# Strassen's seven products for most pairs of MLP up tiles in a two-layer float32 encoder

## The chip, the cores and the metric

One Trainium2 chip (trn2), one core of it. The metric is the device time of one execution in microseconds. Before the change three runs took 1248.66, 1249.28 and 1248.66 us, median 1248.66. TensorE (PE in the profile) multiplies matrices, VectorE (DVE) and ScalarE (ACT) work element by element, GpSimd (POOL) and SyncE (SP) here set buffers and issue DMAs.

## The reference

A two-layer encoder on 512 tokens of 1024 channels, in float32. Each layer normalises x, projects it, runs four mixers side by side (an S5 state-space scan, a convolution module and two kinds of attention), projects their outputs back into x, and then runs the gated MLP that this change is about:

```python
h = rms_norm(x, attn_norm_g[i])
proj = h @ w_in[i]                      # four mixers read slices of proj
...
x = x + mixed @ w_out[i]
h = rms_norm(x, ffn_norm_g[i])
x = x + conv_ffn(h, ffn_w_up[i], ffn_conv_w[i], ffn_conv_b[i], ffn_w_down[i])

def conv_ffn(h, w_up, conv_w, conv_b, w_down):
    u = depthwise_conv(h @ w_up, conv_w, conv_b)      # width 3 over the tokens
    gate, up = jnp.split(u, 2, axis=-1)
    return (jax.nn.silu(gate) * up) @ w_down
```

w_up has 1024 x 5632 values a layer, w_down 2816 x 1024. A last RMSNorm closes the trunk.

## The kernel before

**Layout.** x lies transposed in SBUF, as eight tiles of 128 channels x 512 tokens (`xs_`). A weight tile is the stationary operand, 128 x 128 of it at a time; a tile of activations, 512 tokens wide, is the moving one. All large products are made in three TensorE products of the type fp32r: each operand is split into a rounded part hi and a remainder lo, and hi*hi, hi*lo and lo*hi are summed in PSUM (`mm3`). A weight tile is loaded by SyncE, its hi is a copy by ScalarE or VectorE (`copy` leaves the choice to the planner), its lo a VectorE subtraction (`wget`).

**The MLP** (`ffn`, from line 1392). 44 up tiles a layer, in 22 pairs of one gate and one up tile. `up_tile` takes 8 slices of channels x 3 products of 512 columns into one PSUM bank. The moving operand is x times the norm's gain; the norm's reciprocal root r, which is the same for all channels of a token, is multiplied in when the bank is read (`evac_r`), so that products start before r is known. Then come the conv (one ScalarE operation with the middle tap and the bias, two VectorE taps), Silu of the gate, the product of both, and its split into hi and lo (`pair`). The down projection (`down`) runs in parts of the 22 tiles, `PARTS = (5, 6, 6, 5)`: for each part, eight output tiles with 3 products per tile of the part, each ending in an addition to x by VectorE. A part's down products are recorded after the second pair of the next part. The last part of layer 1 (`finish`) runs in two halves of 256 tokens, with the last norm and the stores behind each half. In layer 0 each pair is followed by a piece of `s5_prep`, small VectorE operations that prepare constants of the next layer's scan.

**The order of the work.** The program first records all instructions and then issues them in the order of a list schedule (`_Plan`). `_cost` (from line 547) gives each instruction a duration, `LAT` the delay between engines; `forward` picks for each engine, in simulated time, the ready instruction with the highest priority (its distance to the end), and lets it start only where its buffers fit. Ten passes are made, forward and backward in turn, and the shortest is issued. At run time each engine works off its list strictly in that order; waits between engines follow from the data and the buffers.

**Buffers.** SBUF has an arena of `NSLOT` = 49 slots of 515 words a partition, one of `NBIG` = 19 slots of 1024 words, and small ones. `CAPS` limits how many raw, hi and lo weight tiles may live at once (3, 5, 5). PSUM has eight banks of 512 words. All waits of SyncE's queue for a free slot hold the loads behind them.

Of the kernel before, what the change touches and what calls it, by code (L numbers as in the profile page):

```python
# [17 lines left out]
P = 128  # L18
# [3 lines left out]
KT = D // P  # L22
DFF = 2816
NPAIR = DFF // P
PARTS = (5, 6, 6, 5)
OUTP = ((3,), (0, 1, 2))
CAPS = (3, 5, 5)
ORDER = ("SGCMpsgcym", "SGCMsgcym")
EARLY = (4, 5)
CONV_PE = ((True, True), (True, False))  # L30
# [22 lines left out]
    CST[_n] = (_off, _w)  # L53
    _off += _w
CSTW = _off
NSLOT = 49
NBIG = 19
SLOTW = S + 3
XW = S + 32
# [7 lines left out]
class _Ap:  # L67
# [17 lines left out]
        return self._do("bitcast", d)  # L85

    def window(self, dims, offset):
        """A view with its own strides."""
        return _Ap(self.base, self.chain + (("window", (dims, offset), {}),), _window(self.proto, dims, offset))

    def unsqueeze(self, d):
# [27 lines left out]


class _Plan:
    """Records instructions, then issues them in the order of a list schedule.

    Buffers live in arenas of SBUF and in the banks of PSUM from their first write to their last use;
    Tile derives every wait from the order of issue."""

    SETS = {"Exp": "exp", "Ln": "ln", "Tanh": "exp", "Sigmoid": "sig", "Silu": "silu", "Gelu_apprx_tanh": "gelu",
            "Sin": "silu"}
# [69 lines left out]
        return op  # L198

    def tiled(self, mms):  # L200
        """Matrix products in column tiles of the array, which run side by side."""
        d = max(_cost("T", *m)[4] for m in mms) + 53.0 * (len(mms) - 1)
        return self.add([("T", "group", mms, {}, d, 0.0, 0.0)])

# [35 lines left out]
            b.at = at  # L240

    def settle(self):
        """Classes of the buffers where the instructions run in the order of recording."""
        left, users, home = dict(self.limit), {}, {}
        for op in self.ops:
            for b in op.bufs:
                users[b] = users.get(b, 0) + 1
        for op in self.ops:
            for b in op.bufs:
                if b not in home:  # L250
                    home[b] = "b" if b.space == "s" and not left["s"] else b.space
                    left[home[b]] -= 1
                    if left[home[b]] < 0:
                        raise RuntimeError("the buffers do not fit: " + home[b])
            for b in op.bufs:
                users[b] -= 1
                if not users[b]:
                    left[home[b]] += 1
        return home
# [45 lines left out]
        return tail  # L305

    def forward(self, prio, ref, home, horizon):
        """One list schedule. ref is an order that fits the buffers: an instruction may run ahead of it
        only where the rest of ref still fits, so that no schedule gets stuck."""
        import bisect  # L310
        import heapq

# [45 lines left out]
            return z <= a or int(load[c][a:z].max()) + k <= limit[c]  # L358

        def fits(op):  # L360
            """The classes for the buffers that op would take, or None."""
            got, need, upto = [], {}, {}
            lag = pos[op.idx] - head
            for b in op.outs:
# [183 lines left out]
def _cost(e, fn, a, k):  # L548
    n = _free(a[0])
    dma = 0.0  # L550
    if e == "T":
        if fn == "transpose":
            d = 109.0
        elif a[1].proto.dtype == F32R:
            d = max(n, 256) / 2.4 + 3.0
        else:
            d = 4.0 * max(n, 128) / 2.4 + 4.0
    elif e == "V":
        ps_ = any(_psum(z) for z in a)
        if fn == "tensor_reduce":  # L560
            d = 65.0 + 1.04 * _free(a[1])
        elif fn == "reciprocal":
            d = 70.0 + 8.0 * n
        elif fn == "memset":
            d = 60.0 + 0.5 * n
        elif fn == "tensor_copy":
            d = 65.0 + (1.04 if ps_ else 0.52) * n
        elif fn == "tensor_scalar":
            d = (125.0 if isinstance(a[2], _Ap) else 65.0) + (1.04 if ps_ else 0.52) * n
        elif fn == "scalar_tensor_tensor":  # L570
            d = (130.0 if isinstance(a[2], _Ap) else 68.0) + 1.04 * n
        else:
            d = 68.0 + 1.04 * n
    elif e == "A":
        d = (65.0 if _psum(a[1]) else 95.0) + 0.82 * n
        if isinstance(k.get("bias"), _Ap):
            d += 90.0
        if isinstance(k.get("scale"), _Ap):
            d += 90.0
        if "accum_out" in k:  # L580
            d += 90.0
    elif e == "G":
        d = 110.0 + (2.0 if fn == "scalar_tensor_tensor" else 1.3) * n
    else:
        d = 470.0 if a[0].shape[0] == P and a[1].shape[0] == P else 640.0
        dma = max(90.0, a[0].shape[0] * n * 4 / 359.0)
    return (e, fn, a, k, d, (2000.0 + dma) if dma else 0.0, dma)
# [3 lines left out]
def trunk_kernel(  # L591
# [30 lines left out]
    xs_ = const.tile([P, KT, S], F32, name="xs_")  # L622
    fing_ = const.tile([P, KT], F32, name="fing_")
    vec_ = const.tile([P, L, VECW], F32, name="vec_")
    slots = ctx.enter_context(tc.tile_pool(name="slots", bufs=1))
    banks = [psp.tile([P, S], F32, name=f"bank{i}") for i in range(8)]
    plan = _Plan(tc, slots, {"s": NSLOT, "b": NBIG, "t": 16}, banks, c_sb)
# [29 lines left out]
    for k in range(KT):  # L657
        lead.append(X.dma_start(x[k], xT[k * P:(k + 1) * P, :]))
    fing = plan.fixed(fing_[:, :])
    X.dma_start(fing, fin_g)  # L660

    vecs = {}
# [8 lines left out]

    def wget(src, n, cap=True):
        raw = sb(F32, (P, n), ("raw", CAPS[0]) if cap else None)
        hi = sb(F32R, (P, n), ("whi", CAPS[1]) if cap else None)
        lo = sb(F32R, (P, n), ("wlo", CAPS[2]) if cap else None)
        plan.loaded = X.dma_start(raw, src)
        copy(hi, raw)
        V.tensor_sub(lo, raw, hi.bitcast(F32))
        return hi, lo
# [38 lines left out]
        return acc  # L718

    def colsum(acc, mat=None):  # L720
        """Sums over the partitions, in every partition."""
        p_ = ps(acc.shape)
        T.matmul(p_, ones if mat is None else mat, acc)
        return p_
# [375 lines left out]
        return [v_[:, :, 0:64], v_[:, :, 64:128]]  # L1100

    def attend(scores, vt):
        """Two heads; their outputs side by side in the partitions."""
        pt = [[b4(F32, (P, 2, S)) for _ in range(2)] for _ in range(2)]
        tot = tiny((P, 4, 2))
        for hh in range(2):
# [31 lines left out]
        return y  # L1138

    def group_norm(l, grp, y):  # L1140
        """y is the group, but twice that for group 0."""
        r = rstd(sumsq(y), 1024 if grp == 0 else 256)
        g, o = tiny((P, 2)), VEC["mix_g"][0] + 2 * grp
        V.tensor_scalar(g, vecs[l][:, o:o + 2], 1.0 if grp else 0.5, None, ALU.mult)
# [12 lines left out]
    def mixing(l):  # L1157
# [224 lines left out]
        for grps in OUTP:  # L1382
# [3 lines left out]
            for m in range(KT):  # L1386
# [2 lines left out]
                mm3(p_, w, range(n), mh, ml, P, P)  # L1389
                V.tensor_add(x[m], x[m], p_)  # L1390

    def ffn(l, side):
        xh, xl, r = prenorm(l, "ffn_g")
        fw, _ = VEC["fc_w"]
        fb, _ = VEC["fc_b"]

        def up_tile(i):
            w = wget(w_up[l, i], KT * P)
            p_ = ps()
            mm3(p_, w, range(KT), xh, xl, P, P)  # L1400
            u = evac_r(p_, r)

            def cw(k):
                return vecs[l][:, fw + 3 * i + k:fw + 3 * i + k + 1]

            y = s2()
            A.activation(y, u, AF.Identity, scale=cw(1), bias=vecs[l][:, fb + i:fb + i + 1])
# [2 lines left out]
            return y  # L1410

        def pair(j):
            g_ = up_tile(2 * j)
            u_ = up_tile(2 * j + 1)
            A.activation(g_, g_, AF.Silu)
            V.tensor_mul(g_, g_, u_)
            return split(g_)
# [11 lines left out]
                V.tensor_add(x[m], x[m], p_)  # L1429

        def finish(k0, n):
            """The last part of the last layer and the norm after it, in two halves of the tokens."""
            ph = {k: prods[k0 + k][0] for k in range(n)}
            pl = {k: prods[k0 + k][1] for k in range(n)}
            H = S // 2
# [22 lines left out]
        pend = None  # L1458
        for n in PARTS:
            for j in range(n):  # L1460
                prods.append(pair(base + j))
                next(side, None)
                if j == 1 and pend is not None:
# [162 lines left out]
```

## Time and profile before

| | before |
|---|---|
| median of three runs | 1248.66 us |
| span of the profiled execution, first to last instruction | 1248.9 us |
| mean granted TensorE clock | 0.998 |
| busy: PE, DVE, ACT, POOL | 1222.4, 926.8, 615.2, 6.9 us |
| TensorE products | 5824 |
| HBM read | 118.96 MB |

The page gives no time of the profiled execution beside its span; the span stands for it. PE's busy time counts pipelined products from start to modelled end, so that a busy PE need not be at its fastest; the count of products in a window gives their rate. "PEld" are weight loads, which overlap products. The rows of a group end with the idle time just before its instructions and what ended it. Nearly every instruction is issued by one helper, so that all rows carry the line L527 and are told apart by operation, shape and buffer: `bank` is PSUM, `v_s` a slot of the small arena, `v_b` of the large one, `xs__65` is x, `vec__67` the vector of gains and taps, `c_sb` constants. The MLP of layer 0 lies at about 267 to 640 us, that of layer 1 from about 870 us to the end. A few per cent of the product records can be missing.

### The profile page before, as it was taken

What the parts mean: (1) busy time and instruction counts of PE and PEld (TensorE: products, weight loads), DVE (VectorE), ACT (ScalarE), POOL (GpSimd) and SP (SyncE); (2) the same over time, 40 slices, a digit from 0 to 9 for tenths busy, and PEclk for the clock granted to TensorE, in tenths of its full rate; (3) what the DMA queues carried; (4) which work ended last, traced back from release to release, by engine and by line L of the source; (5) the groups of instructions that cost most, each with busy time, mean ns of one, the idle gap of its engine ahead of it and who ended that gap; (6) DMA issues with size and microseconds to landing.
All of it is one profiled execution on the core that took longest, in us unless ns stands there. A gap on an engine that the chain in (4) does not pass through costs nothing.

```text
span 1248.9 us, 15868 instructions
## 1 busy us (share of the span) xinstructions
PE 1222.4 (98%) x5824; PEld 937.8 (75%) x5824; DVE 926.8 (74%) x1706; ACT 615.2 (49%) x983; POOL 6.9 (1%) x27
## 2 busy tenths in 40 slices
PE   7999899999999999999999999999999999999996
PEld 5875456878888878888888756668888888888886
DVE  8889988868899665665677998887666656557465
ACT  6448689654443352333352666985533333234223
POOL 0000000000000000000000000000000000000000
PEclk9999999999999999999999999999999999999999
DMA  8559461332223332432555156234223332322211
GB/s 303 148 187 268 107 156 36 134 119 89 71 77 101 101 131 92 123 95 73 187 188 179 53 140 148 64 102 133 87 67 99 109 96 89 99 102 76 83 45 68
DMA packets 71662, 144.38 MB, mean 116 GB/s; under 512 B 20256, under 2 KB 28960, under 8 KB 71456
## 3 DMA queue, kind: packets, MB, share of 16 engines
q1 hardware_dynamic: 71584, 143.37, 37.5%
q8 instruction: 46, 0.75, 0.2%
q14 instruction: 32, 0.26, 0.1%
HBM read 118.96 MB, written 13.89 MB: 106 GB/s over the span
## 4 chain that ended last, share of the span: by engine, by line
PE 88%; DVE 5%; ACT 3%; DMA 1%; issue 1%; SPq 1%; ACTq 0%; DVEq 0%
PE bank L527 88%; DVE v_s L527 4%; ACT v_s L527 2%; DVE v_b L527 1%; DMA v_b<-v_b 1%; ACT L527 1%; SPq L527 1%; ACT v_b L527 1%; DVE v_t L527 0%; DMA xs__65<-in_xT_dram 0%; DMA v_s<-y_d 0%; ACTq L1621 0%; DVEq L1621 0%; ACTq L527 0%
## 5 line engine op out<-in xcount | busy, mean ns | idle before, releaser
L527 PE MATMUL bank<-v_s,v_b 128*128 128x512 f32 (+3 forms) x4594 | 1041.0, 396 | 11.6 <-ACT v_b L527 8.6
L527 PEld LDWEIGHTS bank<-v_s,v_b 128*128 128x128 f32 (+2 forms) x4594 | 794.8, 183 | 219.4 <-issue 25.7
L527 DVE TENSOR_TENSOR v_b<-v_b,v_b 128x1024 fp32r<-128x1024 f32 (+4 forms) x208 | 217.2, 1051 | 33.2 <-PE bank L527 18.2
L527 ACT CAST v_b<-v_b 128x1024 fp32r<-128x1024 f32 (+2 forms) x184 | 168.8, 934 | 114.8 <-PE bank L527 85.1
L527 DVE TENSOR_TENSOR v_s<-v_s,v_s 128x512 f32<-128x512 f32 (+6 forms) x294 | 179.9, 627 | 26.1 <-ACT v_s L527 23.2
L527 DVE TENSOR_TENSOR v_s<-bank,v_s 128x512 f32<-128x512 f32 (+1 forms) x119 | 83.0, 701 | 139.6 <-PE bank L527 137.5
L527 ACT ACTIVATE v_s<-v_s,vec__67 128x512 f32<-128x512 f32 x87 | 71.0, 817 | 195.3 <-DVE v_s L527 192.2
L527 DVE SCALAR_TENSOR_TENSOR v_s<-v_s,vec__67,v_s 128x511 f32<-128x511 f32 (+8 forms) x201 | 148.6, 746 | 15.3 <-ACT v_s L527 9.7
L527 ACT ACTIVATE v_s<-v_s 128x512 f32<-128x512 f32 (+2 forms) x124 | 71.1, 587 | 80.3 <-DVE v_s L527 79.4
L527 DVE TENSOR_TENSOR xs__65<-xs__65,bank 128x512 f32<-128x512 f32 x88 | 59.5, 682 | 61.5 <-PE bank L527 61.5
L527 ACT CAST v_s<-v_s 128x512 fp32r<-128x512 f32 (+1 forms) x70 | 40.0, 585 | 72.9 <-DVE v_s L527 71.4
L527 ACT ACT_TABLE_LOAD x52 | 66.7, 1283 | 15.7 <-DVE v_s L527 7.6
L527 PE MATMUL bank<-v_b,v_b 96*128 96x512 f32 (+5 forms) x264 | 74.1, 450 | 0.0
L527 PE MATMUL bank<-c_sb,v_s 128*128 128x128 f32 x368 | 64.8, 278 | 1.3 <-ACT v_s L527 1.2
L527 PEld LDWEIGHTS bank<-c_sb,v_s 128*128 128x128 f32 x368 | 44.6, 140 | 27.5 <-issue 18.5
L527 PE MATMUL bank<-v_b,v_s 128*128 128x64 f32 (+4 forms) x268 | 60.7, 393 | 1.9 <-ACT v_s L527 1.2
L527 PE MATMUL bank<-v_s,v_s 128*64 128x128 f32 (+2 forms) x258 | 57.4, 348 | 1.4 <-ACT v_s L527 1.4
L527 ACT ACTIVATE v_s<-bank,v_t 128x512 f32<-128x512 f32 x68 | 46.5, 697 | 10.6 <-DVE v_t L527 10.5
L527 PEld LDWEIGHTS bank<-v_b,v_s 128*128 128x128 f32 (+1 forms) x268 | 34.0, 173 | 16.0 <-issue 7.7
L527 DVE TENSOR_REDUCE v_t<-bank 128x1 f32<-128x512 f32 x64 | 42.3, 681 | 4.4 <-PE bank L527 3.7
L527 PEld LDWEIGHTS bank<-v_b,v_b 96*128 96x128 f32 (+3 forms) x264 | 33.2, 165 | 16.5 <-issue 8.1
L527 PEld LDWEIGHTS bank<-v_s,v_s 128*128 128x128 f32 (+1 forms) x258 | 32.1, 165 | 14.9 <-issue 5.7
(82 smaller groups left out, 517.9 us busy)
## 6 DMA issues: line engine op xcount, KB each, us to landing
v_b<-in_w_up_dram SPq DMA_DIRECT2D x88, 512.0 KB
v_b<-in_w_in_dram SPq DMA_DIRECT2D x28, 512.0 KB
v_b<-in_w_dn_dram SPq DMA_DIRECT2D x32, 384.0 KB
v_b<-in_w_dn_dram SPq DMA_DIRECT2D x32, 320.0 KB
v_b<-v_b SPq DMA_DIRECT2D x24, 256.0 KB
v_b<-in_w_out_dram SPq DMA_DIRECT2D x16, 384.0 KB
v_s<-x_d SPq DMA_DIRECT2D x22, 257.5 KB
v_s<-wt_d SPq DMA_DIRECT2D x15, 256.0 KB
```

Source lines behind the costliest of these rows:

```text
L527: self.issued(op, getattr(eng[e], fn)(*[res(z) for z in a], **{n: res(z) for n, z in k.items()}))
```

## The change

19 of the 22 pairs of a layer (all but the first three) are computed by one level of Strassen's scheme, in the variant with chained sums. The pair of tiles (2 x 128 outputs), the 1024 channels and the 512 tokens are each halved: A is the weight in four blocks of 128 outputs x 512 channels, B the normalised activations in four blocks of 512 channels x 256 tokens. Seven block products of 4 x 3 TensorE products with 256 columns take the place of eight.

- **Weights of a pair.** SyncE loads five blocks of 128 x 512 words (two of them into the targets of sums), GpSimd adds a further block to each of two of these by a DMA with addition, VectorE makes two more sums (`s2_`, `s4`). The seven operands are split into hi and lo.
- **Activations.** Once a layer, recorded after the first pair, `operands` makes the four blocks of x times gain times r, four combinations of them, and splits all seven. r must be known for these.
- **Sums of the products.** Three banks: `xb` takes products 1, 4, 6 and 7 on top of each other and is read after each, `yb` takes 3 and 5, `zb` takes 2. Four reads are ScalarE copies, three are VectorE additions, all 256 wide. The up tile comes out with its sign reversed, and so takes negated conv taps (`nfw`, made once a layer).
- **The first three pairs** stay as they are, but with weights in blocks of 512 words instead of 1024.
- **Limits.** `PARTS` becomes (4, 4, 4, 4, 3, 3); `NSLOT` 50; `WCAPS` limits the raw, hi and lo blocks that live at once to 10, 9 and 9.
- **Planner.** The duration of an fp32r product becomes 0.4453 ns a column (at least 256) + 4 ns, before 1/2.4 + 3; a DMA of GpSimd gets a duration.

```diff
-PARTS = (5, 6, 6, 5)
+PARTS = (4, 4, 4, 4, 3, 3)
+DIRECT = 3
...
+WCAPS = (10, 9, 9)
...
-NSLOT = 49
+NSLOT = 50
...
-            d = max(n, 256) / 2.4 + 3.0
+            d = 0.4453 * max(n, 256) + 4.0
...
+    elif e == "G" and fn == "dma_start":
+        d, dma = 1300.0, 2.0 * a[0].shape[0] * n * 4 / 359.0
...
+        def operands():
+            q = {}
+            for kh, nh in ((0, 0), (0, 1), (1, 0), (1, 1)):
+                t_ = q[kh, nh] = b4(shape=(P, 4, H))
+                for k in range(4):
+                    V.scalar_tensor_tensor(t_[:, k], x[4 * kh + k][:, H * nh:H * nh + H], vcol(l, "ffn_g", 4 * kh + k),
+                                           r[:, H * nh:H * nh + H], ALU.mult, ALU.mult)
+            b11, b12, b21, b22 = q[0, 0], q[0, 1], q[1, 0], q[1, 1]
+            n1, n2, t4 = (b4(shape=(P, 4, H)) for _ in range(3))
+            V.tensor_sub(n1, b11, b12)
+            f11 = halves(b11)
+            V.scalar_tensor_tensor(n2, n1, -1.0, b22, ALU.mult, ALU.subtract)
+            fn1 = halves(n1)
+            V.scalar_tensor_tensor(t4, n2, -1.0, b21, ALU.mult, ALU.subtract)
+            f21, fn2 = halves(b21), halves(n2)
+            V.tensor_sub(b12, b22, b12)
+            return dict(b11=f11, b21=f21, n1=fn1, n2=fn2, b22=halves(b22), t3=halves(b12), t4=halves(t4))
+
+        def product(out, w, f, start):
+            for k in range(4):
+                sl = slice(k * P, k * P + P)
+                T.matmul(out, w[0][:, sl], f[0][:, k], start=start and k == 0, stop=False, skip_group_check=True)
+                T.matmul(out, w[0][:, sl], f[1][:, k], start=False, stop=False, skip_group_check=True)
+                T.matmul(out, w[1][:, sl], f[0][:, k], start=False, stop=(k == 3), skip_group_check=True)
+
+        def quarters(j):
+            src = {(i, h): w_up[l, 2 * j + i, :, 512 * h:512 * h + 512] for i in range(2) for h in range(2)}
+            a0, a1, c1, s1, s2_, s3, s4 = (sb(F32, (P, 512), ("sw", WCAPS[0])) for _ in range(7))
+            for t_, z in ((s1, (1, 0)), (s3, (0, 0)), (a0, (0, 0)), (a1, (0, 1)), (c1, (1, 1))):
+                X.dma_start(t_, src[z])
+            GP.dma_start(s1, src[1, 1], accum_op=ALU.add)
+            GP.dma_start(s3, src[1, 0], accum_op=ALU.add)
+            V.tensor_add(s2_, s1, a0)
+            V.tensor_add(s4, s2_, a1)
+            w11, w12, w1, w2, w4, w3, w22 = (halves(z, *CW) for z in (a0, a1, s1, s2_, s4, s3, c1))
+            g_, u_ = s2(), s2()
+            xb, yb, zb = (ps((P, H)) for _ in range(3))
+            product(xb, w11, ops["b11"], True)
+            A.activation(g_[:, 0:H], xb, AF.Copy)
+            product(zb, w12, ops["b21"], True)
+            V.tensor_add(g_[:, 0:H], g_[:, 0:H], zb)
+            product(yb, w1, ops["n1"], True)
+            A.activation(u_[:, H:S], yb, AF.Copy)
+            product(xb, w2, ops["n2"], False)
+            A.activation(g_[:, H:S], xb, AF.Copy)
+            product(yb, w4, ops["b22"], False)
+            V.tensor_add(g_[:, H:S], g_[:, H:S], yb)
+            product(xb, w3, ops["t3"], False)
+            V.tensor_add(u_[:, H:S], u_[:, H:S], xb)
+            product(xb, w22, ops["t4"], False)
+            A.activation(u_[:, 0:H], xb, AF.Copy)
+            return g_, u_
...
         def pair(j):
-            g_ = up_tile(2 * j)
-            u_ = up_tile(2 * j + 1)
+            g_, u_ = straight(j) if j < DIRECT else quarters(j)
+            g_ = spread(2 * j, g_, False)
+            u_ = spread(2 * j + 1, u_, j >= DIRECT)
             A.activation(g_, g_, AF.Silu)
             V.tensor_mul(g_, g_, u_)
             return split(g_)
...
         for n in PARTS:
             for j in range(n):
+                if base + j == 1:
+                    ops = operands()
                 prods.append(pair(base + j))
```

`halves` splits a tile into hi and lo, `straight` is the old up tile with its weights in halves, `spread` the conv with plain or negated taps.

More of the change, by code (lines that the diff above doesn't have):

```diff
@@ L624, in trunk_kernel @@
     vec_ = const.tile([P, L, VECW], F32, name="vec_")
+    nfw_ = const.tile([P, 6 * NPAIR], F32, name="nfw_")
     slots = ctx.enter_context(tc.tile_pool(name="slots", bufs=1))
@@ L659, in trunk_kernel @@
     fing = plan.fixed(fing_[:, :])
+    nfw = plan.fixed(nfw_[:, :])
     X.dma_start(fing, fin_g)
@@ L673, in wget, with halves @@
         raw = sb(F32, (P, n), ("raw", CAPS[0]) if cap else None)
-        hi = sb(F32R, (P, n), ("whi", CAPS[1]) if cap else None)
-        lo = sb(F32R, (P, n), ("wlo", CAPS[2]) if cap else None)
         plan.loaded = X.dma_start(raw, src)
+        return halves(raw, ("whi", CAPS[1]) if cap else None, ("wlo", CAPS[2]) if cap else None)
+    def halves(raw, ch=None, cl=None):
+        hi, lo = sb(F32R, raw.shape, ch), sb(F32R, raw.shape, cl)
         copy(hi, raw)
@@ L1390, in mixing, with blocks @@
                 V.tensor_add(x[m], x[m], p_)
+    def blocks(l, j):
+        w = [[sb(F32, (P, 512), ("sw", WCAPS[0])) for _ in range(2)] for _ in range(2)]
+        for i in range(2):
+            for h in range(2):
+                X.dma_start(w[i][h], w_up[l, 2 * j + i, :, 512 * h:512 * h + 512])
+        return w
     def ffn(l, side):
@@ L1395, in ffn @@
         fb, _ = VEC["fc_b"]
[L1397 to L1401, printed above, removed]
+        V.tensor_scalar(nfw, vecs[l][:, fw:fw + 6 * NPAIR], -1.0, None, ALU.mult)
+        H = S // 2
+        CW = ("sh", WCAPS[1]), ("sl", WCAPS[2])
+        def operands():
[15 more added lines that the diff above has]
+            return dict(b11=f11, b21=f21, n1=fn1, n2=fn2, b22=halves(b22), t3=halves(b12), t4=halves(t4))
@@ new lines, in straight @@
+        def straight(j):
+            out = []
+            for w in blocks(l, j):
+                w = [halves(z, *CW) for z in w]
+                p_ = ps()
+                for k in range(KT):
+                    sl = slice(k % 4 * P, k % 4 * P + P)
+                    wh, wl = w[k // 4]
+                    T.matmul(p_, wh[:, sl], xh[k], start=(k == 0), stop=False)
+                    T.matmul(p_, wh[:, sl], xl[k], start=False, stop=False)
+                    T.matmul(p_, wl[:, sl], xh[k], start=False, stop=(k == KT - 1))
+                out.append(evac_r(p_, r))
+            return out
@@ L1403, in cw, with spread @@
+        def spread(i, u, neg):
             def cw(k):
-                return vecs[l][:, fw + 3 * i + k:fw + 3 * i + k + 1]
+                z = 3 * i + k
+                return nfw[:, z:z + 1] if neg else vecs[l][:, fw + z:fw + z + 1]
             y = s2()
```

## The prediction

> **What bounds the kernel now.** I read the page's busy shares and chain of waits first, then windows of the MLP stage, then the groups of instructions with shapes kept apart, and last the timeline where VectorE runs without a pause.
>
> ```profile
> span 1248.9 us, 15868 instructions
> PE 1222.4 (98%) x5824; PEld 937.8 (75%) x5824; DVE 926.8 (74%) x1706; ACT 615.2 (49%) x983; POOL 6.9 (1%) x27
> PE 88%; DVE 5%; ACT 3%; DMA 1%; issue 1%; SPq 1%; ACTq 0%; DVEq 0%
> ...
> core 0: us, PE busy (x) PEld busy (x) DVE busy (x) ACT busy (x) POOL busy (x), PEclk, DMA share, GB/s
> 100.00:150.00 50.00, 47.24 (x307) 21.70 (x306) 49.40 (x157) 36.23 (x65) 0.48 (x4) 1.00 0.77 209
> 300.00:400.00 100.00, 100.00 (x432) 80.95 (x432) 90.72 (x205) 42.33 (x67) 1.78 (x5) 1.00 0.24 78
> 900.00:1000.00 100.00, 100.00 (x433) 80.91 (x432) 65.16 (x86) 37.51 (x50) 0.00 (x0) 1.00 0.30 93
> 880.00:1200.00 320.00, 320.00 (x1381) 258.94 (x1380) 198.63 (x261) 114.51 (x148) 0.00 (x0) 1.00 0.29 90
> ```
>
> TensorE makes 88% of the chain that ends last. In the MLP of layer 1 (880 to 1200 us) it never pauses, at the full granted clock of 1.00: 320 / 1381 = 231.7 ns for a product of 512 columns. VectorE has 38% of that time free. The row 300 to 400 lies in the MLP of layer 0, where VectorE also prepares the next layer's S5 constants: it is 91% busy, and TensorE still starts 432 products against 433 in layer 1. So on this plan a VectorE at 91% costs TensorE nothing. At 99% (100 to 150 us) TensorE does show gaps.
>
> **TensorE.** A pair now costs 2 x 8 x 3 = 48 products of 512 columns; a Strassen pair 7 x 4 x 3 = 84 of 256. This shape runs already, in the last step of the kernel, with the same order of hi, hi, lo weights and a weight load for each:
>
> ```profile
> 1209.75 19.56 PE L527 MATMUL bank<-v_s,v_b 128*128 128x256 f32 x164
> L527 PE MATMUL bank<-v_s,v_b 128*128 128x256 f32 x240 | 30.4, 282 | 0.0
> 1209.75:1229.31 19.56, 19.56 (x167) 19.56 (x166) 10.78 (x25) 4.54 (x11) 0.00 (x0) 1.00 0.00 1
> 1212.00:1220.00 8.00, 8.00 (x70) 8.00 (x69) 5.16 (x12) 2.45 (x6) 0.00 (x0) 1.00 0.00 0
> ```
>
> The run of 164 ends with the last one's own 0.28 us, of which 0.12 would be its slot: (19.56 - 0.16) / 164 = 118.3 ns. Bounds: 8.00 / 70 = 114.3 (the count holds products begun before the window) and 19.56 / 164 = 119.3. A pair goes from 48 x 231.7 = 11.12 us to 84 x 118.3 = 9.94, that is 1.18 us less (1.10 to 1.52 by the bounds). 38 pairs: **45.0 us** (42 to 58). A layer's MLP on TensorE, with 528 products of the down projection, goes from 1584 x 231.7 = 367 us to 672 x 231.7 + 1596 x 118.3 = 344.5.
>
> In that last step the weight loads are busy for 19.56 of 19.56 us, against 81 of 100 us with 512 columns: at 256 columns the load is nearly as long as the product. The Trainium skill, "TensorE: Matmul & The Clock Gate" (LDWEIGHTS; and under Part 3, what overlaps), gives 128 columns of weights 107 ns and says that a load overlaps running products only when its row group differs. By that rule as it stands a product of 256 columns would take over 213 ns and the change would lose some 38 x (84 x 0.213 - 11.12) = 257 us. The trace differs, with 118.3 ns in this same shape, so I give that outcome no more than 1 in 100, within the 0.07 of the accumulates below.
>
> **VectorE.** Mean durations, and the interval at which independent instructions follow each other:
>
> ```profile
> L527 DVE TENSOR_TENSOR v_b<-v_b,v_b 128x1024 fp32r<-128x1024 f32 x114 | 138.4, 1217 | 7.5 <-PE bank L527 6.3 <-issue 0.4 <-ACT v_b L527 0.2
> L527 DVE SCALAR_TENSOR_TENSOR v_s<-v_s,vec__67,v_s 128x511 f32<-128x511 f32 x166 | 122.7, 747 | 11.5 <-ACT v_s L527 9.7
> L527 DVE TENSOR_TENSOR v_s<-v_s,v_s 128x512 f32<-128x512 f32 x154 | 103.5, 685 | 6.4 <-ACT v_s L527 4.0 <-PE bank L527 0.9
> L527 DVE TENSOR_TENSOR v_s<-xs__65,bank 128x256 f32<-128x256 f32 x16 | 6.4, 418 | 8.3 <-PE bank L527 8.3
> ...
> 1013.73 2.35 DVE L527 TENSOR_TENSOR v_b<-v_b,v_b 128x1024 fp32r<-128x1024 f32 x2
> 1211.24 0.74 DVE L527 SCALAR_TENSOR_TENSOR v_s<-v_s,vec__67,v_s 128x511 f32<-128x511 f32 x1
> 1211.91 0.68 DVE L527 TENSOR_TENSOR xs__65<-xs__65,bank 128x512 f32<-128x512 f32 x1
> 1212.50 0.69 DVE L527 TENSOR_TENSOR v_s<-v_s,v_s 128x512 f32<-128x512 f32 x1
> 1218.01 0.42 DVE L527 TENSOR_TENSOR v_s<-xs__65,bank 128x256 f32<-128x256 f32 x1
> 1218.34 1.48 DVE L527 TENSOR_TENSOR v_s<-v_s,v_s 128x256 f32<-128x256 f32 x3
> 1241.99 3.25 DVE L527 SCALAR_TENSOR_TENSOR v_s<-v_s,fing__66,v_s 128x256 f32<-128x256 f32 x8 [2.27 <-ACT v_s L527]
> ```
>
> Intervals: 0.60 us for a 512-wide two-tensor operation (1211.91 to 1212.50), 0.67 for a conv tap, 2.35 - 1.22 = 1.13 at 1024, 0.33 for a 256-wide add from PSUM, 0.40 for a 256-wide scale. Each is about 0.08 under the mean duration. Now, a layer takes 44 x (1.13 + 0.60 + 2 x 0.67) + 22 x 1.2 + 45 for down = 206 us by intervals, or 229 with 284 x 0.08 added; the window gives 198.63 / 320 x 367 = 228. So unpressed VectorE counts mean durations, and the intervals are what it can be pressed to.
>
> A Strassen pair has 11 operations 512 wide (2 weight sums, 7 lo parts, the product, its lo part), 3 adds from PSUM and 4 taps: 6.6 + 1.0 + 2.7 = 10.3 us, against 7.3 for a pair now. A layer then has 19 x 10.3 = 196; 3 straight pairs of 8 operations and 4 taps, 22; down in six parts, 32 lo parts of 512 and 16 of 384 columns (0.47 from the slope) and 48 adds to x, 19 + 8 + 29 = 56 (45 before, so six parts cost 11); the seven operands, 16 scales, 4 combinations and 7 lo parts, 6 + 5 + 8 = 19; the norm 10. Sum **303 us by intervals**, 303 + 516 x 0.08 = 344 by durations, for 344.5 us of TensorE. Layer 0 has the S5 preparation on top: 90.72 - 65.16 = 25.6 in one window and about 3 before it, so 331 (372).
>
> Layer 1 is thus at 88%, below the 91% that the trace shows as free: nothing lost in its steady part. Layer 0 is at 96%. If 91% is all that TensorE tolerates, the stage takes 331 / 0.907 = 365 and loses 20 us; at 98.8% it loses nothing. I take 95%: 348, **4 us**. At each start three straight pairs (33 us of TensorE) must cover the norm's reciprocal root (some 5 us) and, on VectorE, evacuations and weight halves (3 x 3.6), operands (19) and the first halves: 5 + 11 + 19 + 1 = 36. **3 us a layer**, 0 to 8; the taps of the straight pairs can wait.
>
> At the end the last part has 3 tiles, not 5. The last pair's chain of evacuation, conv, Silu, product and split (about 6 us by the durations above) is covered by the other tiles of that part in eight banks: 8 x 2 x 3 x 0.118 = 5.7 us, before 11.3. **2 us**, 0 to 4.
>
> **ScalarE and PSUM.**
>
> ```profile
> L527 ACT CAST v_s<-v_s 128x512 fp32r<-128x512 f32 x59 | 36.3, 620 | 71.7 <-DVE v_s L527 71.4
> L527 ACT ACTIVATE v_s<-v_s,vec__67 128x512 f32<-128x512 f32 x87 | 71.0, 817 | 195.3 <-DVE v_s L527 192.2 <-issue 2.9
> L527 ACT COPY v_s<-bank 128x224 f32<-128x224 f32 x7 | 2.4, 347 | 7.2 <-PE bank L527 3.1 <-DVE v_s L527 2.6 <-issue 1.5
> ```
>
> A pair: 8 casts, 2 conv starts, 4 copies out of PSUM (0.37 each) and a Silu (0.63): 8.7 us; with down 10 of 15.5 us. No bound. Within a pair, product 4 waits for the copy that read product 1's bank, and product 7 follows product 6 in the same bank behind a VectorE add, some 1 us. Down tiles and the next pair's first product are there to fill it. Cost 0; without them 1 us x 38.
>
> **DMAs.** SyncE issues 5 loads of 256 KB a pair and GpSimd 2 that add to them; 2.25 MB per 15.5 us with down, against 1.5 MB in 16.7 us at a DMA share of 0.29. No accumulating DMA exists before. The nearest row is a plain load that a cast waited for:
>
> ```profile
> 1169.73 0.33 SPq L527 DMA_DIRECT2D v_b<-in_w_dn_dram  x1
> 1172.91 0.84 ACT L527 CAST v_b<-v_b 128x768 fp32r<-128x768 f32 x1 [1.75 <-DMA v_b<-in_w_dn_dram]
> POOL v_b L527 <- PE bank L527: 382.8, 6, 183.4
> ```
>
> 384 KB take 3.2 us from issue to use. An accumulate is at least that and, reading its target too, I bound it at twice, 6.4; so a sum is ready 6 to 10 us after its first load. Ten slots for 7 raw tiles a pair let one live 10 x 15.5 / 7 = 22 us, so I take 0. If late, the weight add at the head of VectorE's in-order queue holds the taps, splits and evacuations behind it, and TensorE with them. GpSimd's queue also holds memsets that wait long for their buffers (last row); an accumulate behind one waits too. The Trainium skill, "DMA: Bandwidth & Descriptors" (Anatomy of one DMA), has 2.0 us + bytes / 436e3, by which 256 KB is 2.6 us and the sum stays as it is; no run here shows it.
>
> **Sum.** 1248.9 - 45.0 + 4 + 6 + 2 = **1216 us**. The profiled span equals the median of the runs (1248.66) within 0.02%, so I carry it over.
>
> **Rivals.** *Full gain*: everything is hidden, 1248.9 - 45 = 1204, at the low price of a product 1191. For it: the free 91% row; against it: layer 0 at 96%.
> *VectorE becomes the bound* (slower): it works off its queue at mean durations because each pair's adds, taps and splits hang on each other. Then layer 0 needs 372 us and layer 1 344; with 5% of waits 392 + 362 = 754 against 734 now: 1269. It decides from the point where VectorE's achieved price per operation passes about 0.05 us over the interval in both layers. For it: the unpressed windows count durations; against it: 90.72 of 100 with TensorE unhurt.
> *Accumulates set the pace* (slower): GpSimd's queue takes two a pair one after the other; over 7.75 us each they are slower than TensorE's 15.5. At 8.5 us: 38 x 1.5 = 57 more than the forecast, 1273. Against it: 3.2 us for the plain load.
> *The new TensorE price mostly reorders*: the planner's list changes in every stage, and what is won in the MLP is given back in mixing. TensorE's idle time is only 26.5 us in all (1248.9 - 1222.4), so some 10 us either way around the forecast, with 30 at the far end: 1246.
>
> **How the numbers follow.** Forecast (1209 to 1230) 0.50, full gain 0.17, VectorE bound, wholly or in part (1230 to 1269), 0.20, accumulates 0.07, reordering 0.06. Of VectorE's 0.20, 0.08 stays faster, 0.04 lands within 0.2%, 0.08 is slower; the last two give 0.05 faster, 0.02 same, 0.06 slower. A measurement of this kernel can tell about 0.2% (2.5 us) from no change. So faster 0.80, same 0.06, slower 0.14. The range runs from 1201 (full gain with a little of the lower product price) to 1248.
>
> **What would show it.** In MLP windows about 118 ns per product of 256 columns and TensorE busy throughout in layer 1; VectorE near 90% in layer 1, above 93% in layer 0. Wrong if TensorE's waits in the MLP name VectorE for more than about 25 us together, if VectorE waits for an accumulating DMA, or if 256-column products come slower than 120 ns.

## The result and the profile after

The changed kernel takes 1284.24 us (median of four runs, 1282.14 to 1286.61) against 1248.97 of the kernel before on the same chip (1248.66 to 1250.99). The ratio is 1.0275 with a 95% interval of 1.0255 to 1.0295: 2.7% slower. The prediction was 1216 us, faster, with a range up to 1248. The profiled execution took 1286.61 us with a span of 1284.8, at a mean granted clock of 0.965.

From the page of the changed kernel, the span, the busy shares and the clock in 40 slices of 32 us:

```profile
span 1284.8 us, 20243 instructions
PE 1213.8 (94%) x7144; PEld 986.5 (77%) x7144; DVE 1101.0 (86%) x2167; ACT 751.7 (59%) x1363; POOL 73.0 (6%) x103
PEclk9999699999997959999999999999999999999998
```

TensorE is idle for 71.0 us instead of 26.5, and the clock leaves its full value in slices 5, 13 and 15. To see where, the span is cut into its four stages: mixing and MLP of layer 0, mixing and MLP of layer 1. The border between two stages is ScalarE's last split of x for the norm that opens the later one; the first 15 us are left out. Columns are the window, its length, busy time and count of PE, PEld, DVE, ACT and POOL, the granted clock, the DMA share and GB/s. The windows of before:

```profile
15.00:266.30 251.30, 247.33 (x1296) 167.19 (x1295) 220.92 (x498) 169.35 (x306) 3.24 (x11) 1.00 0.52 156
266.30:646.60 380.30, 380.30 (x1686) 305.98 (x1685) 276.04 (x478) 152.96 (x228) 2.83 (x7) 1.00 0.34 109
646.60:870.40 223.80, 220.14 (x1131) 157.43 (x1130) 190.94 (x371) 144.92 (x252) 0.48 (x4) 1.00 0.42 119
870.40:1248.90 378.50, 368.47 (x1704) 302.88 (x1702) 229.16 (x324) 138.00 (x186) 0.00 (x0) 0.99 0.27 86
```

and of the changed kernel:

```profile
15.00:281.50 266.50, 256.18 (x1295) 171.12 (x1294) 227.74 (x524) 166.41 (x299) 6.08 (x14) 0.96 0.52 150
281.50:689.20 407.70, 374.68 (x2383) 334.09 (x2382) 351.72 (x683) 224.63 (x430) 33.17 (x42) 0.94 0.52 142
689.20:924.20 235.00, 229.21 (x1119) 158.85 (x1118) 196.61 (x384) 149.74 (x256) 3.98 (x8) 0.99 0.42 112
924.20:1284.80 360.60, 347.59 (x2340) 318.15 (x2338) 315.24 (x546) 201.08 (x368) 29.48 (x34) 0.99 0.48 126
```

| stage | before | predicted | after | after - before |
|---|---|---|---|---|
| mixing, layer 0 | 251.3 | 251.3 | 266.5 | +15.2 |
| MLP, layer 0 | 380.3 | 364.8 | 407.7 | +27.4 |
| mixing, layer 1 | 223.8 | 223.8 | 235.0 | +11.2 |
| MLP, layer 1, and end | 378.5 | 361.0 | 360.6 | -17.9 |

The predicted column is the prediction's own terms put to their stages: 22.5 us of TensorE off each MLP, 3 us for its start, 4 more in layer 0, 2 at the end. Layer 1 comes out as forecast, though in part by errors that cancel: TensorE's busy time there fell by 20.9 us (368.47 to 347.59) where 22.5 were forecast, and its idle time grew by 3.0 where start and end were to cost 5. Layer 0's MLP misses by 43 us, and the two mixing stages, in which not one operation was changed, lose 26.

**Layer 1: the price of a product holds.** The longest run of 256-column products on the timeline of the changed kernel:

```profile
978.99 10.87 PE L529 MATMUL bank<-v_b,v_s 128*128 128x256 f32 x90
```

With the last product's slot taken off as in the prediction, (10.87 - 0.16) / 90 = 119.0 ns. The 107 ns that the Trainium skill ("TensorE: Matmul & The Clock Gate", LDWEIGHTS; Part 3, what overlaps) would put beside each product is not there; the trace contradicts that rule, as the prediction assumed. The group of these products has almost no idle time ahead of it in 925 to 1250 us:

```profile
L529 PE MATMUL bank<-v_b,v_s 128*128 128x256 f32 x1532 | 256.3, 281 | 2.1 <-ACT v_s L529 1.4 <-DVE xs__65 L529 0.5
```

The adding DMAs, which no row of before could price, from the DMA part of the page and the view of their tile, and the one wait of VectorE for any such weight:

```profile
v_s<-in_w_up_dram POOLq DMA_DIRECT2D x70, 256.0 KB, 4.8
DMA to landing us min/median/max: 3.9/4.6/9.1
DVE v_b L529 <- DMA v_b<-in_w_up_dram: 0.6, 1, 0.6
```

A median of 4.6 to 4.8 us from issue to landing lies inside the bounds of 3.2 to 6.4, but the slowest took 9.1; the 2.6 us quoted beside these bounds is under even the fastest, 3.9. VectorE waited 0.6 us for them in layer 0 and not at all in layer 1.

**Layer 0: two gaps.** Five windows of 20 us of its MLP, in the changed kernel:

```profile
361.00:381.00 20.00, 19.53 (x131) 17.77 (x130) 19.98 (x60) 12.31 (x26) 1.93 (x4) 1.00 0.52 139
381.00:401.00 20.00, 8.37 (x36) 6.81 (x35) 19.16 (x59) 7.97 (x16) 3.12 (x4) 0.73 0.53 132
421.00:441.00 20.00, 20.00 (x134) 18.26 (x132) 16.48 (x30) 9.37 (x20) 2.26 (x3) 1.00 0.30 69
441.00:461.00 20.00, 9.03 (x44) 7.06 (x42) 15.21 (x25) 8.96 (x23) 2.28 (x3) 0.59 0.40 111
461.00:481.00 20.00, 13.64 (x59) 8.93 (x59) 11.76 (x18) 5.02 (x16) 0.53 (x1) 0.50 0.17 58
```

The two gaps differ. In the first (381 to 401) VectorE is full; in the second (441 to 481) it is busy 27 of 40 us (15.21 + 11.76). The timeline of the first gap, TensorE's rows and then VectorE's (start, duration, operation, count, idle time before it and what ended it):

```profile
383.77 3.05 PE L529 MATMUL bank<-v_s,v_s 128*128 128x512 f32 x12 [0.95 <-DVE v_s L529]
397.50 2.72 PE L529 MATMUL bank<-v_b,v_s 128*128 128x256 f32 x11 [10.68 <-DVE xs__65 L529]
...
392.27 0.74 DVE L529 SCALAR_TENSOR_TENSOR v_s<-v_s,nfw__68,v_s 128x511 f32<-128x511 f32 x1
392.93 0.22 DVE L529 TENSOR_TENSOR v_b<-v_b 128x64 f32<-128x64 f32 x1
393.12 0.69 DVE L529 TENSOR_TENSOR v_b<-v_b,v_s 128x512 f32<-128x512 f32 x1
393.73 0.22 DVE L529 TENSOR_TENSOR v_b<-v_b 128x64 f32<-128x64 f32 x1
396.76 0.68 DVE L529 TENSOR_TENSOR xs__65<-xs__65,bank 128x512 f32<-128x512 f32 x1
```

TensorE waits 10.68 us for an addition to x that empties a bank. Ahead of that addition VectorE's list alternates MLP operations with the narrow ones (16 to 64 columns) of the S5 preparation. Second gap, TensorE and then SyncE's queue:

```profile
447.55 2.07 PE L529 MATMUL bank<-v_s,v_s 128*128 128x512 f32 x4 [5.44 <-DVE xs__65 L529]
470.79 1.97 PE L529 MATMUL bank<-c_sb,v_s 128*128 128x128 f32 x8 [5.51 <-ACT v_b L529]
...
419.31 21.82 SPq L529 DMA_DIRECT2D v_s<-in_w_up_dram  x6
451.71 3.00 SPq L529 DMA_DIRECT2D wt_d<-v_s  x2
479.89 1.11 SPq L529 DMA_DIRECT2D k_d<-v_b  x1
481.57 0.37 SPq L529 DMA_DIRECT2D v_s<-in_w_up_dram  x1
```

Six up weight loads are spread over 22 us to 441.1, and the next one is issued at 481.57. Between them SyncE's queue has nothing but the preparation's stores to scratch (`wt_d`, `g_d`, `k_d`) and, from 479.5 us, two loads for down. The queue itself stands for most of these 40 us: by its waits some 25 us for results that these stores take (10.5 before the first `wt_d`, 6.1 before the `k_d` at 470.40), and 8.6 us for TensorE, before the first load for down. The up loads come behind all of this in its list. TensorE starts no 256-column product from 441.6 to 483.5 us and does a few products of 512 columns and the preparation's small ones, one dependent step at a time. In this stretch the granted clock falls to 0.59 and 0.50, so that what TensorE does there takes longer as well.

### The profile page after: what moved, and what is told of

Read it like the earlier page. It is cut to its first block, busy times and chain, and to the rows that moved or that the text cites. A ratio compares the mean times of both kernels' runs of the same rounds, so it can differ in the third digit from the quotient of the medians.

```text
span 1284.8 us, 20243 instructions
## 1 busy us (share of the span) xinstructions
PE 1213.8 (94%) x7144; PEld 986.5 (77%) x7144; DVE 1101.0 (86%) x2167; ACT 751.7 (59%) x1363; POOL 73.0 (6%) x103
## 5 line engine op out<-in xcount | busy, mean ns | idle before, releaser
L529 PE MATMUL bank<-v_b,v_s 128*128 128x256 f32 (+3 forms) x3350 | 579.0, 294 | 25.9 <-DVE xs__65 L529 11.2
L529 PEld LDWEIGHTS bank<-v_b,v_s 128*128 128x128 f32 (+1 forms) x3350 | 476.5, 189 | 56.8 <-ACT v_s L529 14.7
L529 PE MATMUL bank<-v_s,v_s 128*128 128x512 f32 (+2 forms) x1462 | 441.0, 386 | 7.1 <-DVE xs__65 L529 5.4
L529 DVE TENSOR_TENSOR v_s<-v_s,v_s 128x512 fp32r<-128x512 f32 (+6 forms) x622 | 393.3, 656 | 33.7 <-ACT v_s L529 13.7
L529 PE MATMUL bank<-v_s,v_b 128*128 128x512 f32 (+3 forms) x1510 | 360.3, 421 | 11.0 <-ACT v_b L529 8.6
L529 PEld LDWEIGHTS bank<-v_s,v_s 128*128 128x128 f32 (+1 forms) x1462 | 259.2, 187 | 64.0 <-issue 6.2
L529 ACT CAST v_s<-v_s 128x512 fp32r<-128x512 f32 (+2 forms) x371 | 215.5, 605 | 156.5 <-PE bank L529 79.9
L529 PEld LDWEIGHTS bank<-v_s,v_b 128*128 128x128 f32 (+2 forms) x1510 | 225.9, 176 | 93.1 <-issue 34.2
L529 PE MATMUL bank<-v_b,v_b 128*128 128x256 f32 (+5 forms) x382 | 113.4, 398 | 4.9 <-DMA v_b<-v_b 2.0
L529 DVE SCALAR_TENSOR_TENSOR v_s<-v_s,vec__67,v_s 128x511 f32<-128x511 f32 (+9 forms) x131 | 97.2, 746 | 8.6 <-ACT v_s L529 6.4
```

The source lines that it names most:

```text
L529: self.issued(op, getattr(eng[e], fn)(*[res(z) for z in a], **{n: res(z) for n, z in k.items()}))
```

## The experiments

The theories: (A) VectorE is too full in layer 0; (B) the S5 preparation and the seven operands together hold too many buffers, so that the list lets the MLP's weights wait until the preparation is done; (C) in the mixing stages it is the order of the list alone, with or without the new price. Stages below are in the order of the table above. The letters in the recorded expectations are others: there A is the preparation's sharing of VectorE and slots (A and B here), split into A1 (slots, B here) and A2 (a full VectorE, A here); B is adding DMAs that come late, C a gain that was an accident, D the new price, and E is C here. Stage lengths come from one profiled execution of each kernel, and executions of one kernel lie 0.3 to 11 us apart, so a stage difference of a few us carries little.

**The preparation moved out of layer 0's MLP.** It is recorded in layer 1's mixing instead, and there with ordinary priority; beside the MLP its priority was lowered (the -1e6 in the edit).

```diff
-ORDER = ("SGCMpsgcym", "SGCMsgcym")
+ORDER = ("SGCMpsgcym", "SGCMpsgcym")
...
-            if l == 0:
-                for _ in s5_prep(0):
+            if 1:
+                for _ in s5_prep(l):
...
-        ffn(l, s5_prep(l + 1, -1e6) if l + 1 < L else iter(()))
+        ffn(l, iter(()))
```

> The preparation of layer 1's S5 constants is taken out of the MLP of layer 0 and recorded in the mixing of layer 1, right before the scan that uses it; all else as in the changed kernel. Theory A (the loss in layer 0 comes from this preparation sharing VectorE and SBUF slots with the Strassen pairs): the MLP of layer 0 falls from 408 us to 350 to 360, TensorE keeps its full clock there, the mixing of layer 1 grows from 235 to 245 to 260, the whole lands at 1235 to 1255. Theory B (the adding DMAs come late and starve TensorE): layer 0's MLP stays above 385 and the whole above 1270.

1239.6 us, 0.9908 of before (0.9883 to 0.9933): 0.9% less than the kernel before, and 3.5% less than the changed one. Stages 252.8, 353.1, 257.4, 360.1. Layer 0's MLP in this run:

```profile
267.75:620.86 353.11, 350.67 (x2280) 317.26 (x2279) 322.48 (x609) 204.93 (x374) 29.63 (x36) 1.00 0.51 138
```

Without the preparation beside it, layer 0's MLP has no gap, at the full clock. The mixing that now holds it grows by 33.6 us over before, so the preparation is not free there. It shows that the preparation is part of the cause, but fits A and B alike; adding DMAs that starve TensorE are out, since they are all still there.

**Strassen in layer 1 alone.** Layer 0's MLP is that of before.

```diff
         def pair(j):
-            g_, u_ = straight(j) if j < DIRECT else quarters(j)
+            if l == 0:
+                g_ = spread(2 * j, up_tile(2 * j), False)
+                u_ = spread(2 * j + 1, up_tile(2 * j + 1), False)
+            else:
+                g_, u_ = straight(j) if j < DIRECT else quarters(j)
...
-        for n in PARTS:
+        for n in (PARTS if l else (5, 6, 6, 5)):
```

> Strassen pairs, six parts and adding DMAs only in layer 1; the MLP of layer 0 is that of the kernel before, with the preparation beside it. Theory A: layer 0's MLP is back at 380 us, layer 1's stays at 361. If the two mixing stages stay as long as in the changed kernel (266 and 235) the whole is 1257; if they were long because of what surrounds them and go back to 251 and 224, it is 1231. Theory C (Strassen pairs gain nothing in themselves, and the 361 us are an accident): layer 1's MLP is back near 378 and the whole at or above 1249.

1240.17 us, 0.9908 (0.9888 to 0.9928). Stages 250.6, 380.2, 234.0, 359.4. Layer 1 gives 19.1 us, so its gain is no accident of one list; layer 1's mixing takes 10.2 of it back although none of its operations was changed, only the planner's price of a product.

**Before with the new price, and after with the old one.**

```diff
-            d = max(n, 256) / 2.4 + 3.0
+            d = 0.4453 * max(n, 256) + 4.0
```

> The kernel before with only the planner's new price of a TensorE product. Theory D (the new price makes the mixing stages longer): the mixing stages go from 251 and 224 us to about 266 and 235, the whole to about 1275. If the price does nothing but reorder: 1249 plus or minus 5.

> The changed kernel with the old price of a TensorE product. Theory D: mixing back at 251 and 224 us, the whole near 1258. Otherwise the mixing stages stay near 266 and 235 and the whole near 1284.

Before with the new price: 1264.28, 1.0105 (1.0065 to 1.0146). Its MLPs stay (379.4, 378.4); its mixing goes to 259.6 and 233.8, +8.3 and +10.0 (of its two executions, 1260.49 and 1268.07, the profiled one is the longer). After with the old price: 1290.05, 1.0311 (1.0271 to 1.0351), with stages 275.0, 400.5, 232.2, 369.2. So the new price does lengthen the mixing of the old kernel, but the old price does not shorten that of the new one; the first mixing even takes 8.5 us more, in an execution 3.6 us above that kernel's median. The first total lies between the two that were expected, 1249 and 1275. The price is not the cause as such. Layer 0's MLP keeps its excess under either.

**A against B, first: fewer operands.** In layer 0 alone three of the seven split operands stand in for the others, so that 8 of 14 large buffers are free; this leaves out four of the operands, so that layer 0's products have their number and shape but not all of their data. The preparation stays in its place.

```diff
-            f21, fn2 = halves(b21), halves(n2)
+            f21, fn2 = (halves(b21), halves(n2)) if l else (f11, fn1)
             V.tensor_sub(b12, b22, b12)
+            if l == 0:
+                f3 = halves(b22)
+                return dict(b11=f11, b21=f11, n1=fn1, n2=fn1, b22=f3, t3=f3, t4=f3)
```

> The changed kernel, but in layer 0 only three of the seven split activation operands are made and used in turn for the seven products (so layer 0's MLP computes something else). This frees 8 of the 14 large slots that the operands hold through the stage; the products, the weight sums and splits and the S5 preparation stay; VectorE saves only four splits once, 4.5 us. Theory A1 (the preparation and the pairs jam on SBUF slots): layer 0's MLP falls from 408 us to 350 to 362, with the preparation still beside it. Theory A2 (VectorE is too full in layer 0): it stays above 390.

1240.58 us, 0.992 (0.990 to 0.994). Stages 261.1, 360.4, 242.2, 360.0. From its windows:

```profile
276.07:636.50 360.43, 357.44 (x2340) 321.30 (x2339) 342.21 (x677) 213.47 (x408) 32.21 (x41) 1.00 0.55 149
290.00:390.00 100.00, 100.00 (x689) 92.58 (x688) 99.53 (x191) 64.05 (x118) 11.22 (x13) 1.00 0.64 164
440.00:480.00 40.00, 39.60 (x286) 36.97 (x285) 38.54 (x81) 26.06 (x54) 5.38 (x7) 1.00 0.52 133
```

and its timeline, SyncE's queue:

```profile
444.90 25.56 SPq L529 DMA_DIRECT2D v_s<-in_w_up_dram  x10
505.58 0.33 SPq L529 DMA_DIRECT2D wt_d<-v_s  x1
613.57 0.37 SPq L529 DMA_DIRECT2D wt_d<-v_s  x1
```

VectorE is 95% busy over the stage and 99.5% over 100 us, with TensorE full. So VectorE's load alone does not stop TensorE. With buffers free, the preparation's stores lie spread over 505 to 614 us, and up loads go on through the stretch in which the changed kernel had none. In this list the preparation is not finished as one block.

**A against B, second: a lighter VectorE.** In layer 0 alone, two weight sums a pair are left out, with two SyncE loads into the same buffers in their place. This makes VectorE lighter, but it also puts 38 more loads into SyncE's queue.

```diff
-            V.tensor_add(s2_, s1, a0)
-            V.tensor_add(s4, s2_, a1)
+            V.tensor_add(s2_, s1, a0) if l else X.dma_start(s2_, src[0, 0])
+            V.tensor_add(s4, s2_, a1) if l else X.dma_start(s4, src[0, 1])
```

> The changed kernel, but in layer 0 the two weight sums of VectorE are left out and their targets are loaded by SyncE instead (so layer 0's MLP computes something else). VectorE loses 38 operations of 0.6 us, 23 us, which takes it from 96% to 89% of the stage by my count; the slots stay as they are. Theory A2: layer 0's MLP falls to 350 to 365. Theory A1: it gains some 10 to 15 us from the shorter list and stays above 385.

1261.14 us, 1.0084 (1.0064 to 1.0104). Stages 256.3, 399.2, 230.6, 359.2. Its windows:

```profile
271.33:670.54 399.21, 373.10 (x2383) 331.11 (x2383) 334.31 (x654) 221.53 (x427) 33.03 (x42) 0.97 0.60 170
376.00:396.00 20.00, 19.12 (x149) 18.11 (x148) 18.90 (x50) 13.52 (x31) 3.65 (x5) 1.00 0.66 181
416.00:436.00 20.00, 10.52 (x61) 7.57 (x59) 12.69 (x21) 10.04 (x23) 0.25 (x1) 0.76 0.34 118
436.00:456.00 20.00, 15.79 (x75) 12.15 (x76) 12.83 (x20) 6.39 (x18) 1.14 (x2) 0.68 0.41 122
```

VectorE is at 84% of the stage, less than in the run with few operands, and the stage still takes 399 us. There is no gap with a full VectorE any more (19.12 of 20 us busy at 376 to 396), and a long one is there with VectorE at 64%. SyncE's queue has the same pattern as in the changed kernel: one up load between 416.8 and 452.98 us, and the preparation's stores around it. The changed kernel with the old price has it too, with no up load from 457.0 to 482.33 us. So A fits the first gap, by this run some 8 us of the stage, and B the rest; the 8 us are no clean price, since the added loads and the new order go into them as well.

**The price by stage.** The preparation late, and the old price in the mixing stages; and Strassen in layer 1 alone, with the new price for layer 1's MLP only.

```diff
-            d = 0.4453 * max(n, 256) + 4.0
+            d = TP[0] * max(n, 256) + TP[1]
...
+        TP[:] = 1 / 2.4, 3.0
         mixing(l)
+        TP[:] = 0.4453, 4.0
```

In the second of these the last line applies to layer 1 alone.

> As the run with the preparation moved, and the planner's price of a product is the old one for all work recorded in the mixing stages, the new one in the MLPs. If the new price lengthens the mixing stages only by the order it gives: mixing 251 and 248 us (with the preparation), MLPs 353 and 360, the whole near 1228. If not, it stays at 1239.

> Strassen pairs in layer 1 alone, with the old price for everything but the MLP of layer 1. Mixing 251 and 224 us as before, layer 0's MLP 380, layer 1's 360: the whole 1230. If the order of the whole list shifts anyway, 1235 to 1243.

1245.56 (0.9952, 0.9935 to 0.9968) with stages 261.9, 351.4, 260.1, 358.6, and 1253.68 (1.0026, 1.0007 to 1.0046) with 260.6, 386.0, 231.5, 359.2. Both miss what was expected and are slower than the same kernels with the new price throughout: giving the mixing its old price back does not give its old length back.

**Before with its list disturbed.** One number of the planner is changed, the weight of the order of recording in a priority; the instructions and all prices stay, up to the choice of an engine for a copy.

```diff
-    BETA = 40.0
+    BETA = 42.0
```

> The kernel before with one number of the planner changed (how much the order of recording counts in a priority, 42 instead of 40): same instructions, another order. Theory E (a new order alone moves the mixing stages by some 10 us either way, through pauses of TensorE that drop its clock): mixing stages differ from 251 and 224 us by 3 to 12 us each, the MLPs stay at 380 and 378. Rival (only the Strassen pairs or the price lengthen them): 1249 plus or minus 3, all four stages as before.

1265.01 us, 1.0107 (1.0087 to 1.0128). Stages 262.3, 380.6, 226.8, 378.3. The kernel before, with the same instructions in another order, loses 13.5 us against before's 1251.51 in the same comparison, 11.0 of them in the first mixing. Its windows there:

```profile
100.00:150.00 50.00, 41.35 (x256) 19.40 (x255) 49.19 (x150) 37.05 (x61) 0.49 (x4) 0.92 0.75 187
150.00:200.00 50.00, 49.04 (x258) 29.43 (x257) 34.61 (x60) 36.78 (x76) 0.00 (x0) 0.91 0.45 111
```

and TensorE's largest wait in them (us in total, times, longest):

```profile
PE bank L527 <- ACT v_s L527: 7.1, 4, 3.6
```

In windows of 10 us the clock of this run is 0.59 and 0.56 from 140 to 160 us, after waits of 2.39 and 3.56 us. The changed kernel has a pause at the same place, though one that a transfer ends, by its windows:

```profile
130.00:140.00 10.00, 2.88 (x22) 1.12 (x18) 7.98 (x26) 4.82 (x7) 0.00 (x0) 0.70 0.99 209
140.00:150.00 10.00, 10.00 (x40) 4.32 (x36) 6.32 (x15) 1.92 (x5) 0.00 (x0) 0.50 0.32 85
```

and its timeline:

```profile
138.53 1.19 PE L529 MATMUL bank<-v_b,v_s 128*128 128x512 f32 x2 [7.12 <-DMA v_s<-g_d]
```

where the kernel before has, in its window,

```profile
130.00:140.00 10.00, 9.05 (x48) 4.25 (x48) 9.90 (x40) 3.52 (x9) 0.24 (x2) 1.00 0.69 169
```

The pause of 7.12 us for a transfer from scratch is followed by ten us of which TensorE is busy all, at half clock. Of the 15.2 us that the first mixing lost in the changed kernel, 6.4 are idle time of TensorE (10.3 instead of 4.0) and 8.9 longer busy time. C stands as possible: order alone moves the kernel before by 13.5 us, where the mixing stages of the changed one lost 26.

**The adding DMAs priced.** The preparation late and all four weight sums on VectorE; and the preparation late with the adding DMAs left out.

```diff
-            GP.dma_start(s1, src[1, 1], accum_op=ALU.add)
-            GP.dma_start(s3, src[1, 0], accum_op=ALU.add)
+            c0 = sb(F32, (P, 512), ("sw", WCAPS[0]))
+            X.dma_start(c0, src[1, 0])
+            V.tensor_add(s1, s1, c1)
+            V.tensor_add(s3, s3, c0)
```

> As the run with the preparation moved, but all four weight sums of a pair on VectorE, from an extra block loaded by SyncE; no adding DMA. VectorE gains 38 x 2 operations of 0.6 us, 23 us a layer. If VectorE has that room (303 + 23 = 326 of 344 us): both MLPs within 3 us of 353 and 360. If it then binds: 358 to 370 each, the whole 10 to 20 us longer.

> As the run with the preparation moved, with the adding DMAs left out (so the MLPs compute something else). Theory B (they come late and hold VectorE's queue): both MLPs get shorter by over 5 us. If they are hidden: 353 and 360 within 3 us.

With sums on VectorE 1258.45, 1.006 (1.0044 to 1.0076), stages 253.7, 360.5, 254.6, 371.6: against the same kernel with adding DMAs the MLPs take 7.4 and 11.5 us more. In layer 1 TensorE loses 21.8 us with VectorE at 90% (334.5 of 371.6), so that the prediction's "a VectorE at 91% costs TensorE nothing" holds for its plan and is no rule. Layer 0's MLP bears on A: its window

```profile
268.67:629.14 360.47, 351.48 (x2271) 317.07 (x2270) 339.70 (x636) 209.84 (x381) 0.19 (x2) 1.00 0.39 124
```

has 339.7 us of VectorE work, more than the 334.3 of the run with a lighter VectorE, and takes 39 us less than that run, without the preparation beside it. Without the additions 1259.67, 1.0065 (1.0045 to 1.0085), stages 266.5, 355.0, 260.7, 358.6: the MLPs change by +1.9 and -1.6 us. So the adding DMAs are hidden, and the VectorE sums that they replace are not. Both totals are also moved by the mixing (266.5 against 252.8 in the second), where neither kernel was changed; only the MLP stages are read here.

**The preparation first in layer 1's mixing.** A try at the 33.6 us that it costs there.

```diff
-ORDER = ("SGCMpsgcym", "SGCMpsgcym")
+ORDER = ("SGCMpsgcym", "pSGCMsgcym")
```

> As the run with the preparation moved, but recorded first in layer 1's mixing, ahead of its projections, so that it can start under the last down products of layer 0. Theory A: the MLPs stay at 353 and 360; the mixing of layer 1 gets shorter than 257 us, 245 to 252, the whole 1228 to 1240.

1246.37 us, 0.9953 (0.9939 to 0.9967). Stages 251.3, 353.1, 264.7, 361.3. A miss: layer 1's mixing takes 7.3 us more than with the preparation recorded after four of the mixers' parts, at a clock of 0.95 in both.

## Why the prediction was wrong

**What held.** "45.0 us" off TensorE: the products ran at 119.0 ns instead of 118.3, and layer 1's MLP with its start and end lost 17.9 us where the steps sum to 17.5 (a sum nearer than its terms, as said above). "Layer 1 is thus at 88%": measured 315.24 / 360.6 = 87%. The bounds of the accumulates and the 0 taken for them: 4.8 us, hidden. ScalarE and PSUM at 0: TensorE's waits for ScalarE in layer 1 are the 1.4 us of the group row. The rival of accumulates that set the pace is out by the run without them; VectorE as the bound in both layers is out by layer 1 and by the run with few operands.

**The step that failed first: "Layer 0 is at 96%. [...] I take 95%: 348, 4 us".** The stage took 407.7 us, 43 more than the steps give. The 95% was not the error: with few operands VectorE ran at 95% of the stage and TensorE lost 3.0 of 360.4 us. The error was to treat the S5 preparation as 28 us of VectorE work spread over the stage, with nothing else to it. First, it is not spread: in 361 to 401 us VectorE did 119 operations, about half of them the preparation's narrow ones, and TensorE stood 10.68 us for an addition behind them; the run with a lighter VectorE, whose stage is 407.7 - 399.2 = 8.5 us shorter, puts that at some 8 us. Second, it holds buffers. The prediction counted slots for raw weights only; it never set the seven split operands, which stay alive through the MLP, against the preparation's tiles in the same arenas. The list then finished the preparation as a block of dependent steps, with no up load from 441.1 to 481.57 us. Against the run with few operands, TensorE's idle time is 33.0 instead of 3.0 us and its busy time 374.7 instead of 357.4, for which the rows show one cause, the clock of 0.94 instead of 1.00: 30 + 17 = 47 us, the difference of the two stages (407.7 - 360.4). The three lists with Strassen pairs that have both the seven operands and the preparation in this stage take 399 to 408 us (changed kernel, old price, lighter VectorE); the six in which one of the two is gone take 351 to 361. That the two together are the cause is shown by this; that it is through buffers is argued, from the loads that stop and from what the run with few operands frees.

**The step that failed second: the rival of the new price, "some 10 us either way [...] with 30 at the far end".** Mixing lost 26.4 us, and I had given it a chance of 0.06. The sizing went by TensorE's idle time of 26.5 us as what reordering can move. That bounds a gain, not a loss; and it left the clock out, since before ran at 0.998. The price is not even needed: a changed planner number does half as much to the kernel before (+13.5 us). Over all these lists the first mixing took 250.6 to 275.0 us.

**The tests named beforehand** did not see it. TensorE's largest waits in layer 0's MLP, in the changed kernel:

```profile
PE bank L529 <- DVE xs__65 L529: 16.1, 2, 10.7
PE bank L529 <- ACT v_s L529: 6.8, 6, 3.0
PE bank L529 <- ACT v_b L529: 5.5, 1, 5.5
PE bank L529 <- DVE v_s L529: 3.2, 5, 1.1
PE bank L529 <- DVE v_b L529: 0.9, 1, 0.9
```

VectorE's rows make 20.2 us, below the 25 that were to prove the forecast wrong; 12.3 are under ScalarE's name. VectorE waited 0.6 us for one adding DMA, and the products came at 119 ns. One sign did fail, VectorE "above 93% in layer 0", with 351.72 / 407.7 = 86%, but because the stage was longer and not because VectorE did less. A test for the clock and for loads that stop was missing.

**What stays open.** Whether the list holds the MLP back for slots of the large arena, of the small one, or for its reserve that keeps a schedule from getting stuck was not separated; the run with few operands frees large buffers and lightens VectorE a little at once (342.2 against 351.7 us), and with them the whole order changes. What in an order makes the first mixing 251 or 275 us was not found beyond the pauses shown. In layer 1's mixing, 9.1 of the 11.2 us lost are longer busy time of TensorE (229.21 instead of 220.14) at a clock of 0.99, which neither its pauses nor the clock explain.

## What to carry to other kernels

Where an off-path task shares buffers with a stage, ask what it holds and for how long, not only how many microseconds of an engine it takes; averages of busy time hid both gaps here. In a program whose order comes from a planner, any edit redraws every stage: disturb the old kernel's order once without an edit, and take what that moves (here 13 us of 1250) as the noise that a forecast gain of 33 us must stand against. Of the versions tried, the preparation moved to layer 1's mixing and Strassen in layer 1 alone both take 0.991 of the time before. These 11 us are no more than a change of order moves; what the lists agree on is the stage: layer 1's MLP takes 359 to 361 us in nine of the eleven with Strassen pairs, 369 and 372 in the two others, and 378 in the three lists without.

## What the runs showed of the hardware

A pause of TensorE costs more than its own length. After the 7.12 us wait in the mixing the granted clock was 0.70 and then 0.50 in two windows of 10 us. Cut into 2 us, it was at half from 134 us to about 158, although TensorE had resumed at 138.53 and counts as busy from there on; so the pause put some 24 us under the half clock. And in 441 to 481 us of the MLP it was 0.59 and 0.50 while TensorE was busy 23 of 40 us. The Trainium skill, "TensorE: Matmul & The Clock Gate" (What's actually happening), says that the clock falls to half after an idle window of about 3.4 us; these rows agree with the half. I had left that out. Between its first and its last product the trace of before has no wait of TensorE over 1.4 us from 15 us on; at its end it does show the fall, with the last product over at 1239.7 us, 0.71 in 1243 to 1245 and 0.50 after. The 8.56 us ahead of its first product stand at 1.00.

VectorE can be 99.5% busy for 100 us beside a TensorE that does not pause (290 to 390 us with few operands), while TensorE lost 21.8 us beside a VectorE at 90% in layer 1 with all sums on VectorE. The share alone did not tell which.
